# The low parts of 25 chunks of U made by a negated copy and an adding DMA instead of a subtraction on VectorE

## The chip, the cores and the metric

The kernel runs on one core of one Trainium2 chip. The metric is the time of one execution on the device, in microseconds, the median of three runs: 1719.38 us (1719.3 to 1720.42). Engines are named as in the profile: PE (matrix products), DVE (vector engine), ACT (activations, copies, and one DMA queue), POOL (GpSimd, and the DMA queue whose descriptors software writes), SP (a DMA queue).

## The reference

One decoder block on 512 tokens of width 1024, batch 1, in float32: a token mixer (a causal gated MLP, a sliding-window attention and two sigmoid gates, joined by an output projection) and then a retrieval layer over 16384 single-neuron experts. The change touches the retrieval layer alone:

```
q = (x @ w_pq) -> 8 heads of two halves; s1, s2 = halves . sub_keys      # (t, h, 128) each
v1, i1 = top_k(s1, 16); v2, i2 = top_k(s2, 16)
sc, ci = top_k(v1[..., :, None] + v2[..., None, :], 16)                  # 16 experts of each head
e = i1[ci // 16] * 128 + i2[ci % 16]
g = softmax(sc)
act = gelu(einsum(peer_u[e], x));  out = einsum(g * act, peer_v[e])
```

## The kernel before, in words

The first 459 us are the token mixer. Of the retrieval layer, 384 of the 512 tokens go a dense way: PE multiplies all 16384 rows of `peer_u` (128 chunks of 128 rows, called U here) with the tokens, Gelu is applied, and the result is multiplied with a dense matrix of weights that is zero except at each token's chosen experts; a second product with `peer_v` (V) gives the output. The last 128 tokens go by gathers of their own rows (`gather`, lines 662 to 691).

Every product in float32 precision is made of three products in a reduced format, with each operand split into a high part (the rounded value) and a low part (the rest): `mm3`, lines 59 to 65, issues hi·hi (L62), hi·h2Tlo (L63) and lo·h2Thi (L64) for each of eight slices of a chunk. PE works strictly in its order, so the third matmul of a chunk waits for the chunk's low part, and all behind it too.

The split of a chunk is `load_split2` (lines 445 to 459). SP loads `raw` (four buffers), ACT makes `hi` (three buffers) by a copy that rounds (L450), and the low part (three buffers) is a subtraction. POOL makes it while `last["pool"]` is set (L456), else DVE does (L458):

```
        if last.get("pool"):
            last["pool_lo"] = nc.gpsimd.tensor_sub(lo, raw, hi.bitcast(F32))
        else:
            last["dve"] = nc.vector.tensor_sub(lo, raw, hi.bitcast(F32))
```

`last["pool"]` is on from the query products to the end of the top-k; `end_topk` (line 818) clears it. The stage that follows, "the making of the dense weights", is `spread` (lines 607 to 658): for three tiles of 128 tokens and eight groups of 16 tokens in each, DVE builds four one-hot tensors of 128x2048 in 16 bit (`oh`, L631 to L635), PE multiplies them (32 short matmuls per group into `psg`, L643 and L644), ACT evicts the four results to `stg` (L645) and issues two DMAs that store them to DRAM (`Gd`, L656), and DVE keeps some of them in the resident tile `res` (L651, L653). Meanwhile 25 chunks of U, numbers 33 to 57, are computed as cover (`U_resident` and `U_chunk`, lines 693 to 717); the loop that pairs the two is at lines 858 to 867, five estimated microseconds of `spread` per chunk (`GPUMP`). `end_spread` (line 830) ends it, three more chunks of U follow, and then V.

The order in which each engine takes its instructions is not that of the code: a scheduler places them by its own estimates of when an operand is ready, and the order is fixed in the program. The gathers' first eight loads carry a note that puts them behind the last low part made on POOL (line 670, `behind(d, last["pool_lo"])`, which is an order on POOL's queue and no wait).

Of the kernel before, what the change touches and what calls it, by code (L numbers as in the profile page):

```python
# [8 lines left out]
F32 = mybir.dt.float32  # L9
# [4 lines left out]
AF = mybir.ActivationFunctionType  # L14
ALU = mybir.AluOpType
# [39 lines left out]
def block_kernel(ctx, tc, I, out):  # L55
    nc = tc.nc
# [52 lines left out]
    with ExitStack() as fr:  # L109
# [288 lines left out]
        for hh in range(2):  # L398
            for t in range(NT):
# [13 lines left out]
                for kh in range(2):  # L413
# [5 lines left out]
                    for k4 in range(4):  # L419
                        k = 4 * kh + k4  # L420
                        if k < NEV:
                            nc.scalar.activation(hf[:, k4, :], pt[:, k4 * P:(k4 + 1) * P], AF.Identity,
                                                 scale=G2c[:, k:k + 1], bias=B2c[:, k:k + 1])
# [11 lines left out]
    last = {}  # L435

    def behind(ins, other):

        tc.add_manual_dep(ins.ins, other.ins.name,
                          mybir.DependencyInfo(mybir.DependencyClass.NoSync, mybir.DependencyReason.DATA))  # L440
# [4 lines left out]
    def load_split2(src, nm, pool=None):  # L445
        raw = pw.tile([P, NK * P], F32, name=f"raw{nm}", tag="raw", bufs=4)
        last["dma"] = nc.sync.dma_start(raw, src)
        hi = (pool or pw).tile([P, NK * P], F32R, name=f"hi{nm}", tag="hi", bufs=1 if pool else 3)
        lo = (pool or pw).tile([P, NK * P], F32R, name=f"lo{nm}", tag="lo", bufs=1 if pool else 3)
        h = nc.scalar.activation(hi, raw, AF.Copy)  # L450
        if "expn" in last:
            last["expn"] -= 1
            if last["expn"] == 0:
                behind(last["exp"], h)
        if last.get("pool"):
            last["pool_lo"] = nc.gpsimd.tensor_sub(lo, raw, hi.bitcast(F32))  # L456
        else:
            last["dve"] = nc.vector.tensor_sub(lo, raw, hi.bitcast(F32))  # L458
        return Split(hi, lo)
# [56 lines left out]
    def query(h, half):  # L516
        nm = f"{h}_{half}"
        w = load_split2(I["w_pq"][2 * h + half], f"pq{nm}")
        ps = pu.tile([P, S], F32, name=f"psq{nm}", tag="mm", bufs=2)
        wv = Split(w.hi.rearrange("p (k c) -> p k c", k=NK), w.lo.rearrange("p (k c) -> p k c", k=NK))  # L520
        mm3(ps, [(wv[:, k, :], h2T[:, k, :]) for k in range(NK)])
        qt = tp.tile([P, S], F32, name=f"qt{nm}", tag="qt", bufs=2)
        nc.scalar.copy(qt, ps)
        return qt
# [168 lines left out]
    def U_resident(i):  # L693

        w = load_split2(I["uT"][i], f"U{i}")
        ps = pu.tile([P, SD], F32, name=f"psU{i}", tag="mm", bufs=2)
        wv = Split(w.hi.rearrange("p (k c) -> p k c", k=NK), w.lo.rearrange("p (k c) -> p k c", k=NK))
        last["U"] = mm3(ps, [(wv[:, k, :], h2T[:, k, 0:SD]) for k in range(NK)])
        slot, n = res["tile"][:, len(res["ids"]), :], res["spread"]
        if n < SD:  # L700
            nc.scalar.activation(slot[:, n:], ps[:, n:], AF.Gelu)
        if n:
            a = actp.tile([P, SD], F32, name=f"act{i}", tag="act", bufs=4)
            nc.scalar.activation(a[:, 0:n], ps[:, 0:n], AF.Gelu)
            nc.vector.tensor_mul(slot[:, 0:n], slot[:, 0:n], a[:, 0:n])
        res["ids"].append(i)

    def U_chunk(i, keep_act):
        w = load_split2(I["uT"][i], f"U{i}")
        ps = pu.tile([P, SD], F32, name=f"psU{i}", tag="mm", bufs=2)  # L710
        wv = Split(w.hi.rearrange("p (k c) -> p k c", k=NK), w.lo.rearrange("p (k c) -> p k c", k=NK))
        last["U"] = mm3(ps, [(wv[:, k, :], h2T[:, k, 0:SD]) for k in range(NK)])
        a = actp.tile([P, SD], F32, name=f"act{i}", tag="act", bufs=4)
        nc.scalar.activation(a, ps, AF.Gelu)
        if not keep_act:
            nc.scalar.dma_start(Ad[i], a)
        return a
# [100 lines left out]
    def end_topk():  # L818
        tk.close()
        last["pool"] = PLO > 1  # L820
        res["stack"] = ExitStack()
        rp = res["stack"].enter_context(tc.tile_pool(name="rp", bufs=1, side="right", reuse_waits="tile"))
        res["tile"] = rp.tile([P, NRES, SD], F32, name="res")
        res["ids"] = []
        res["first"] = cur[0] + 1
        res["spread"] = 0
        return
        yield

    def end_spread():  # L830
        done.append(1)
        last["pool"] = False
        return
        yield

    bg += [topk_last(), softmax(), end_topk(), spread(), end_spread()]
    gt = gather()
    n_g = 0
# [140 lines left out]
```

## Time and profile before

| what | us |
|---|---|
| median of three runs | 1719.38 |
| profiled execution, whole | 1727.59 |
| its span, first to last instruction | 1725.9 |
| PE busy in it | 1668.0 (97%) |
| DVE, ACT, POOL busy | 1353.8, 685.9, 481.5 |
| the stage of the change, from the last top-k to the first V chunk | about 720 to 886 |

The profiled execution is 8 us longer than the median of the runs; sums are made within it and their difference is carried to the median. A PE that is busy in the profile is not one at its peak, since matmuls overlap and their ends are modelled: how fast PE goes is read from the distance between the starts of its matmuls.

### The profile page before, as it was taken

To read this page: it belongs to the slowest core of one execution; us is meant where nothing else is said; L and a number is where in the kernel's file an instruction comes from. 1 tells how busy PE (TensorE), PEld (TensorE's weight loads), DVE (VectorE), ACT (ScalarE), POOL (GpSimd) and SP (SyncE) were. 2 spreads that over 40 slices of the span, in tenths; PEclk is the share of its full clock that TensorE was granted. 3 is DMA by queue.
4 is the path that set the end of the run, shared out by engine and by line. 5 is a ranking of instruction groups with operands and counts; after the bars stand their busy time and mean duration, and the time that the engine had idled before them with its cause. 6 is when DMAs were issued, how large, how long until landed. Compare 5 with 4: busy or idle time off the path is not lost.

```text
span 1725.9 us, 23559 instructions
## 1 busy us (share of the span) xinstructions
PE 1668.0 (97%) x8658; PEld 1442.8 (84%) x8658; DVE 1353.8 (78%) x2509; ACT 685.9 (40%) x1095; POOL 481.5 (28%) x334
## 2 busy tenths in 40 slices
PE   6999999999999999899999999999999999989997
PEld 3765777788788999899998789999999999978886
DVE  6467786454589999999978888778787888878787
ACT  3467632233343333355543233333333333333333
POOL 2000000000043455400014444444454545531202
PEclk9999999999999999999999999999999999999999
DMA  7602257642252355556699999999899999899982
GB/s 269 201 1 74 98 196 245 219 146 86 77 189 78 103 173 172 191 206 224 211 321 365 363 325 340 320 338 351 312 337 324 326 345 324 311 351 316 305 282 86
DMA packets 162071, 409.92 MB, mean 238 GB/s; under 512 B 22337, under 2 KB 69473, under 8 KB 161698
## 3 DMA queue, kind: packets, MB, share of 16 engines
q1 hardware_dynamic: 112178, 245.35, 42.3%
q0 software_dynamic: 36960, 134.50, 21.6%
q10 hardware_dynamic: 12816, 28.55, 4.3%
q8 instruction: 68, 1.11, 0.3%
q14 instruction: 49, 0.40, 0.1%
HBM read 377.07 MB, written 31.01 MB: 236 GB/s over the span
## 4 chain that ended last, share of the span: by engine, by line
PE 55%; DVE 18%; DMA 5%; issue 4%; POOL 2%; ACT 0%; SPq 0%; DVEq 0%; POOLq 0%; ACTq 0%
PE acc L801 8%; PE acc L800 8%; PE acc L797 8%; PE psU L64 7%; PE psU L62 6%; PE psU L63 6%; DMA wa<-in_w_ada_dram 2%; POOL ru L667 2%; DMA ru<-in_peer_u_dram,idx 1%; DMA rawV<-in_peer_v_dram 1%; PE pso L63 1%; PE pso L64 1%; PE psga L64 1%; PE psga L62 1%; PE pspa L64 1%
## 5 line engine op out<-in xcount | busy, mean ns | idle before, releaser
L64 PE MATMUL psU<-h2Thi,loU 128*128 128x384 f32 x1008 | 340.6, 338 | 5.4 <-DVE loU L458 5.3
L62 PE MATMUL psU<-h2Thi,hiU 128*128 128x384 f32 x1008 | 340.8, 338 | 0.0
L63 PE MATMUL psU<-h2Tlo,hiU 128*128 128x384 f32 x1008 | 339.3, 337 | 0.0
L797 PE MATMUL acc<-hiV,wh 128*128 128x512 f32 x768 | 300.1, 391 | 4.5 <-ACT wh L782 4.5
L800 PE MATMUL acc<-loV,wh 128*128 128x512 f32 x768 | 301.5, 393 | 1.5 <-DVE loV L458 1.5
L801 PE MATMUL acc<-hiV,wl 128*128 128x512 f32 x768 | 301.1, 392 | 0.3 <-DVE wl L783 0.3
L667 POOL DMA_INDIRECT ru<-in_peer_u_dram,idx x128 | 159.0, 1242 | 360.6 <-DVE ru L671 341.2
L680 POOL DMA_INDIRECT rv<-in_peer_v_dram,idx x128 | 176.4, 1378 | 247.9 <-DVE facc L686 226.6
L458 DVE TENSOR_TENSOR loV<-rawV,hiV 128x1024 fp32r<-128x1024 f32 x128 | 156.4, 1222 | 101.2 <-ACT hiV L450 100.9
L450 ACT ACTIVATE hiV<-rawV 128x1024 fp32r<-128x1024 f32 x128 | 135.1, 1055 | 224.2 <-PE psU L63 184.1
L450 ACT ACTIVATE hiU<-rawU 128x1024 fp32r<-128x1024 f32 x126 | 134.0, 1063 | 194.5 <-PE psU L63 105.5
L64 PEld LDWEIGHTS psU<-h2Thi,loU 128*128 128x128 f32 x1008 | 190.4, 189 | 7.7 <-DVE loU L458 7.6
L63 PEld LDWEIGHTS psU<-h2Tlo,hiU 128*128 128x128 f32 x1008 | 190.6, 189 | 2.6
L62 PEld LDWEIGHTS psU<-h2Thi,hiU 128*128 128x128 f32 x1008 | 190.4, 189 | 2.6
L797 PEld LDWEIGHTS acc<-hiV,wh 128*128 128x128 f32 x768 | 144.9, 189 | 33.7 <-ACT wh L782 5.1
L671 DVE SCALAR_TENSOR_TENSOR ru<-ru,h2n 128x1024 f32<-128x1024 f32 x128 | 154.4, 1221 | 22.0 <-DMA ru<-in_peer_u_dram,idx 21.8
L800 PEld LDWEIGHTS acc<-loV,wh 128*128 128x128 f32 x768 | 144.8, 189 | 32.0 <-DVE loV L458 3.1
L801 PEld LDWEIGHTS acc<-hiV,wl 128*128 128x128 f32 x768 | 144.8, 189 | 31.1 <-DVE wl L783 0.7
L686 DVE SCALAR_TENSOR_TENSOR facc<-rv,wg,facc 128x1024 f32<-128x1024 f32 x126 | 159.4, 1278 | 11.7 <-DMA rv<-in_peer_v_dram,idx 11.7
L456 POOL TENSOR_TENSOR lopq<-rawpq,hipq 128x1024 fp32r<-128x1024 f32 x16 | 40.7, 2544 | 325.1 <-ACT hipq L450 325.1
L782 ACT ACTIVATE wh<-wf 128x384 fp32r<-128x384 f32 x107 | 56.2, 526 | 183.4 <-DVE wf L778 100.5
L458 DVE TENSOR_TENSOR loU<-rawU,hiU 128x1024 fp32r<-128x1024 f32 x95 | 115.7, 1218 | 1.4 <-ACT hiU L450 1.4
(628 smaller groups left out, 2942.4 us busy)
## 6 DMA issues: line engine op xcount, KB each, us to landing
rawU<-in_uT_dram SPq DMA_DIRECT2D x128, 512.0 KB
rawV<-in_peer_v_dram SPq DMA_DIRECT2D x128, 512.0 KB
wa<-in_w_ada_dram SPq DMA_DIRECT2D x48, 512.0 KB
G<-Gd SPq DMA_DIRECT2D x11, 1536.0 KB
Gd<-stg ACTq DMA_DIRECT2D x24, 592.0 KB
rawpq<-in_w_pq_dram SPq DMA_DIRECT2D x16, 512.0 KB
Ad<-act ACTq DMA_DIRECT2D x38, 192.0 KB
ar<-Ad SPq DMA_DIRECT2D x9, 768.0 KB
```

What stands on the lines that cost most here:

```text
L62: nc.tensor.matmul(ps, l.hi, r.hi, start=(i == 0), stop=False)
L63: nc.tensor.matmul(ps, l.hi, r.lo, start=False, stop=False)
L64: last = nc.tensor.matmul(ps, l.lo, r.hi, start=False, stop=(i == n - 1))
L450: h = nc.scalar.activation(hi, raw, AF.Copy)
L458: last["dve"] = nc.vector.tensor_sub(lo, raw, hi.bitcast(F32))
L667: d = nc.gpsimd.indirect_dma_start(out=rows, out_offset=None, in_=I["peer_u"], in_offset=bass.IndirectOffsetOnAxis(ap=idx[:, s:s + 1], axi ...
L671: paced(nc.vector.scalar_tensor_tensor(rows, rows, 1.0, h2n, op0=ALU.mult, op1=ALU.mult, accum_out=wg[:, s:s + 1]))
L680: nc.gpsimd.indirect_dma_start(out=rows, out_offset=None, in_=I["peer_v"], in_offset=bass.IndirectOffsetOnAxis(ap=idx[:, s:s + 1], axis=0))
L686: paced(nc.vector.scalar_tensor_tensor(fa, rows, wg[:, s:s + 1], fa, op0=ALU.mult, op1=ALU.add))
L797: m = nc.tensor.matmul(acc, l.hi, r.hi, start=st, stop=False)
L800: nc.tensor.matmul(acc, l.hi, r.lo, start=False, stop=False)
L801: nc.tensor.matmul(acc, l.lo, r.hi, start=False, stop=sp_)
```

## The change

For chunks whose split is made between `end_topk` and `end_spread`, the low part is made in two steps: ACT writes the negated high part into `lo` (a copy with scale -1), and then POOL issues a DMA that adds `raw` to it, in SBUF, element by element.

```diff
-        if last.get("pool"):
+        if last.get("dma_lo"):
+            nc.scalar.activation(lo, hi.bitcast(F32), AF.Copy, scale=-1.0)
+            last["pool_lo"] = nc.gpsimd.dma_start(lo.bitcast(F32), raw, accum_op=ALU.add)
+        elif last.get("pool"):
             last["pool_lo"] = nc.gpsimd.tensor_sub(lo, raw, hi.bitcast(F32))
...
         res["ids"] = []
+        last["dma_lo"] = True
...
-        last["pool"] = False
+        last["pool"] = last["dma_lo"] = False
```

In the built program 25 subtractions leave DVE, 25 copies (L456 of the new code) join ACT and 25 DMAs (L457) join POOL. The scheduler also orders ACT, PE and DVE anew. In names, `hiU49` is the high part of chunk 49, `stg1_6` group 6 of the second tile of tokens, `psg1_6_3` its fourth product; the number at the end only tells buffers apart. The line numbers of the new code stand three higher from L456 on (an eviction is L648, a store L659, the short matmuls L646 and L647).

First place, ACT around groups 5 and 6 of the second tile. Before:

```order
L645 ACTIVATE stg1_5_7258<-psg1_5_3_7289 128x128x4
L656 DMA Gd_76<-stg1_5_7258 128x528
L656 DMA Gd_76<-stg1_5_7258 128x1184
L450 ACTIVATE hiU51_7582<-rawU51_7580 128x1024
L701 ACTIVATE res_6028<-psU48_7316 128x160
L704 ACTIVATE act48_7342<-psU48_7316 128x224
L645 ACTIVATE stg1_6_7345<-psg1_6_0_7346 128x128x4
L645 ACTIVATE stg1_6_7345<-psg1_6_1_7356 128x128x4
L645 ACTIVATE stg1_6_7345<-psg1_6_2_7366 128x128x4
L645 ACTIVATE stg1_6_7345<-psg1_6_3_7376 128x128x4
```

The same place on ACT after the change:

```order
L648 ACTIVATE stg1_5_7273<-psg1_5_3_7304 128x128x4
L450 ACTIVATE hiU49_7415<-rawU49_7413 128x1024
L659 DMA Gd_76<-stg1_5_7273 128x528
L659 DMA Gd_76<-stg1_5_7273 128x1184
L704 ACTIVATE res_6028<-psU48_7332 128x160
L707 ACTIVATE act48_7358<-psU48_7332 128x224
L648 ACTIVATE stg1_6_7361<-psg1_6_0_7362 128x128x4
L648 ACTIVATE stg1_6_7361<-psg1_6_1_7372 128x128x4
L648 ACTIVATE stg1_6_7361<-psg1_6_2_7382 128x128x4
L648 ACTIVATE stg1_6_7361<-psg1_6_3_7392 128x128x4
L456 ACTIVATE loU49_7416<-hiU49_7415 128x1024
```

Behind group 5 ACT made the high part of chunk 51 before and makes that of chunk 49 now, two chunks later in the sequence; the negated copy of chunk 49 stands behind the four evictions of group 6.

Second place, PE at chunk 49. Before, its 24 matmuls stand together behind group 6:

```order
L644 MATMUL psg1_6_3_7376<-oh2_1_6_7305,oh0_1_6_7303 128x128
L62 MATMUL psU49_7403<-h2Thi_2987,hiU49_7399 128x384
L63 MATMUL psU49_7403<-h2Tlo_2988,hiU49_7399 128x384
L64 MATMUL psU49_7403<-h2Thi_2987,loU49_7400 128x384
L62 MATMUL psU49_7403<-h2Thi_2987,hiU49_7399 128x384
```

Now PE takes two matmuls of the chunk, then the 32 of group 7, and then the other 22, the first of which reads the low part. The two ends of group 7:

```order
L647 MATMUL psg1_6_3_7392<-oh2_1_6_7320,oh0_1_6_7318 128x128
L62 MATMUL psU49_7420<-h2Thi_2987,hiU49_7415 128x384
L63 MATMUL psU49_7420<-h2Tlo_2988,hiU49_7415 128x384
L646 LDWEIGHTS oh0_1_7_7406
L646 MATMUL psg1_7_0_7450<-oh1_1_7_7407,oh0_1_7_7406 128x128
```

```order
L647 LDWEIGHTS oh0_1_7_7406
L647 MATMUL psg1_7_3_7480<-oh2_1_7_7408,oh0_1_7_7406 128x128
L64 MATMUL psU49_7420<-h2Thi_2987,loU49_7416 128x384
L62 MATMUL psU49_7420<-h2Thi_2987,hiU49_7415 128x384
L63 MATMUL psU49_7420<-h2Tlo_2988,hiU49_7415 128x384
```

So between group 6, which ACT must evict ahead of the negated copy, and the first use of the low part, PE has two long and 32 short matmuls to do.

Third place, the end of the stage on POOL. Before, the first gathers (`ru`) follow the low part of chunk 32; now they follow the 25 adding DMAs:

```order
L457 DMA loU55_7950<-rawU55_7947 128x1024
L457 DMA loU56_8036<-rawU56_8033 128x1024
L457 DMA loU57_8122<-rawU57_8119 128x1024
L670 DMA ru0_8344<-in_peer_u_dram,idx_8342 128x1024
L670 DMA ru1_8375<-in_peer_u_dram,idx_8342 128x1024
```

The gathers moved from the start of the stage to its end.

## Rows read from the trace of the kernel before

**Rows 1.** The page's part 4, shares of the chain that ended last, by engine.

```profile
PE 55%; DVE 18%; DMA 5%; issue 4%; POOL 2%; ACT 0%; SPq 0%; DVEq 0%; POOLq 0%; ACTq 0%
```

**Rows 2.** Windows: us, busy time per engine (instructions), PE clock, DMA share, GB/s.

```profile
700.00:720.00 20.00, 18.98 (x111) 18.63 (x109) 19.52 (x49) 9.33 (x12) 6.39 (x3) 1.00 0.37 127
720.00:886.00 166.00, 159.47 (x1397) 153.24 (x1398) 158.39 (x193) 88.63 (x174) 5.87 (x4) 0.98 0.64 229
885.00:910.00 25.00, 25.00 (x125) 22.31 (x124) 18.49 (x28) 10.40 (x16) 9.09 (x8) 1.00 1.06 363
910.00:1000.00 90.00, 85.39 (x375) 70.61 (x374) 75.18 (x114) 29.06 (x38) 45.22 (x37) 0.98 0.98 364
```

**Rows 3.** Waits of PE from 690 to 900: us, times, longest.

```profile
PE psg L643 <- DVE oh L635: 2.6, 3, 1.4
PE psU L64 <- DVE loU L458: 2.5, 2, 2.1
PE ptg L615 <- DVE gs L595: 2.3, 1, 2.3
```

**Rows 4.** Instructions by line from 720 to 886: busy us, mean ns, idle before.

```profile
L645 ACT ACTIVATE stg<-psg 128x512 f32<-128x512 f32 x96 | 49.8, 608 | 13.2 <-PE psg L644 13.2
L458 DVE TENSOR_TENSOR loU<-rawU,hiU 128x1024 fp32r<-128x1024 f32 x28 | 34.0, 1217 | 1.2 <-ACT hiU L450 1.2
L450 ACT ACTIVATE hiU<-rawU 128x1024 fp32r<-128x1024 f32 x25 | 26.7, 1068 | 30.7 <-PE psU L63 26.1 <-DVE oh L634 4.6
L701 ACT ACTIVATE res<-psU 128x240 f32<-128x240 f32 (+19 forms) x21 | 7.4, 354 | 12.4 <-PE psU L64 12.4
```

**Rows 5.** Timeline of PE: start, us, line; two long, two short matmuls.

```profile
760.39 0.33 PE L64 MATMUL psU<-h2Thi,loU 128*128 128x384 f32 x1
760.56 0.33 PE L62 MATMUL psU<-h2Thi,hiU 128*128 128x384 f32 x1
...
763.03 0.22 PE L643 MATMUL psg<-oh,oh 128*128 128x128 f16 x1
763.09 0.22 PE L644 MATMUL psg<-oh,oh 128*128 128x128 f16 x1
```

**Rows 6.** Timeline of ACT, a group's two stores issued.

```profile
845.70 0.81 ACTq L656 DMA_DIRECT2D Gd<-stg  x2
```

**Rows 7.** DMA of the stage, 720 to 886: packets and bytes.

```profile
DMA packets 11966, 37.98 MB, mean 229 GB/s; under 512 B 1321, under 2 KB 1956, under 8 KB 11951
```

**Rows 8.** Chain in order of time: start, us; DMA pieces, issue to use.

```profile
282.28 4.25 DMA wa<-in_w_ada_dram
...
977.79 9.72 DMA ru<-in_peer_u_dram,idx
```

**Rows 9.** Timeline of POOL, the two copies inside SBUF.

```profile
58.94 0.76 POOL L206 DMA_DIRECT2D kd<-kd  x1 [24.52 <-ACT kd L204]
59.69 0.57 POOL L207 DMA_DIRECT2D kd<-kd  x1
```

**Rows 10.** DMA from 57 to 62: share in 40 slices; queue: packets, MB, share.

```profile
DMA  8610000000000000000000000098951049898000
...
q0 software_dynamic: 96, 0.26, 23.9%
```

**Rows 11.** Timeline of POOL, first and last of four gathers issued beside DVE's work.

```profile
720.12 1.76 POOL L667 DMA_INDIRECT ru<-in_peer_u_dram,idx  x1 [10.23 <-DVE idx L664]
...
724.94 1.97 POOL L667 DMA_INDIRECT ru<-in_peer_u_dram,idx  x1 [0.30 <-issue]
```

**Rows 12.** Line L667 in the whole span: ns least, median, most.

```profile
L667 POOL DMA_INDIRECT ru<-in_peer_u_dram,idx x128: 933/1012/1967, 720.1 to 1228.5; - x128
```

**Rows 13.** Timeline of PE about 988: a wait, and matmuls behind it.

```profile
986.88 0.34 PE L63 MATMUL psU<-h2Tlo,hiU 128*128 128x384 f32 x1
990.04 0.44 PE L64 MATMUL psU<-h2Thi,loU 128*128 128x384 f32 x1 [2.82 <-DVE loU L458]
...
991.38 0.50 PE L62 MATMUL psU<-h2Thi,hiU 128*128 128x384 f32 x1
```

## Prediction

> **What bounds the kernel now.** I read first the shares of the chain that ended last [rows 1]: PE has 55%, DVE 18%, DMA 5%. Then the windows about the stage that the change touches [rows 2]. From 720 to 886 PE is busy 159.47 of 166.00 us and DVE 158.39, so both look full. Which of them is late is told by the waits of PE [rows 3]: in all it waited 7.4 us for DVE (2.6 for one-hots, 2.5 for low parts, 2.3 for the softmax), which agrees with the idle time of the windows, 6.5 us in 720 to 886 and 1.0 in 700 to 720. The granted clock of the stage is 0.98, a further 0.02 x 166 = 3.3 us. So the most that a faster DVE can give is 7.5 + 3.3 = 10.9 us, although the change takes three times that off DVE. The reader is to see here that a busy share of 95% on DVE is no measure of what its relief is worth: PE is nearly full beside it.
>
> How fast PE goes is read from starts [rows 5]: a long matmul every 0.17 us, a short one every 0.057. A chunk of U is 24 long ones, 4.15 us; a group of the dense weights is 32 short ones, 1.82 us.
>
> **The change part by part.** Removed: 25 subtractions of 1.217 us [rows 4] on DVE, 30.4 us. At most the 10.9 us above come of it. I take 6: the waits for one-hots and low parts go (5.1), and some of the wait for the softmax, which stood behind two subtractions; the clock's 3.3 us I leave, since new waits of PE would lower it too.
>
> Added on ACT: 25 negated copies. The trace has none; the nearest row is the copy of the same tile that makes the high part, 1.07 us [rows 4], so 26.7 us more on an engine that is busy 88.6 of 166 [rows 2]; with stores issued at 0.81 us for two [rows 6], 24 times, that is 88.6 + 26.7 + 19.4 = 135. ACT as a whole is not the bound.
>
> Added on POOL: 25 DMAs. An issue is bounded by 0.57 [rows 9] and 1.97 us [rows 11]; I take the median of the gathers, 1.0 [rows 12]. Nothing but gathers is queued behind them.
>
> Added on the DMA engines: 25 x 0.524 MB = 13.1 MB to the 37.98 MB of the stage [rows 7], at a share that is 0.64 now [rows 2]. An adding DMA is not in the trace, so I bound its landing. A plain load of 0.524 MB took 4.25 us from issue to use [rows 8]; 0.524 MB at the 364 GB/s of a full ring [rows 2] is 1.44 of it, so 2.8 us are fixed. The only copies inside SBUF, issued by POOL, kept their queue at 23.9% of 16 engines for 5 us with 0.26 MB [rows 9, 10]: 19.1 engine-us, or 2.4 us for 0.524 MB. Low end 2.8 (the transfer itself hidden), high end the 9.7 us of a gather of that size in a full ring [rows 8]. I take 2.8 + 2.4 = 5.2, by the copy that is nearest in kind. At that price 25 of them fill 60 us, a share of 0.36, and the ring would stand at 1.00.
>
> What is late next: the low part itself. Before, it came 1.2 us after the high part, and ACT made the high part up to three chunks ahead. Now the order on PE has to cover the copy, the issue and the landing. In the new order I counted, for each of the 25 chunks, what PE has to do between the last of its groups that ACT must see ahead of the negated copy and the first matmul that reads the low part. That cover is 2 long and 32 short matmuls for chunk 49, the place shown, 2.2 us. It is 4.3 for chunks 39 and 50 (4 long, 64 short); 5.3 for 41; 6.3 for 40 and 48; 6.7 to 7.1 for 38, 42 and 47; 5.9 for 57; 7.3 to 8.6 for 51 to 56; 8.0 to 16 for the other nine.
>
> The chain to be covered has three forms, with 0.61 for the last eviction, 1.07 for a copy [rows 4], 0.81 for two issues [rows 6]:
> - eviction, negated copy, issue, landing: 0.61 + 1.07 + 1.0 + 5.2 = 7.9. Short by 0.8 at 38, 1.1 at 47, 0.5 at 48 (47's wait counts for it), 5.7 at 49.
> - eviction, high part, two issues, negated copy, issue, landing: 9.8. Short by 5.5 at 39 (40 lies within that wait), and by 1.2 to 2.5 at each of 51 to 56, 10.2 in all; since each of these chains begins ahead of the wait before it, a wait serves two of them, 5.1. The same at 57: 3.9, half of it 2.0.
> - after a chunk's result: two activations of 0.35 [rows 4] and then the copy, 8.0 at chunk 50, short by 3.7; at 41 also an eviction, two issues and two high parts, 11.5, short by 6.2 (42 lies within).
>
> Sum 30.6 us. It moves by 9.5 us for each us of landing: six chunks in full, seven by half.
>
> A wait of PE is followed by a slower PE: after 2.82 us for a low part the next matmuls took 0.50 us instead of 0.33, and the clock of that stretch is 0.98 of 90 us, 1.8 us lost [rows 2, 13]. Four new waits are longer than that; I take 4 us (0 to 7).
>
> Moved: the first four gathers go on POOL's queue behind the 25 DMAs, from a stage with a share of 0.64 to the end of it. DVE reads them after the stage, so their latency is hidden, but 2.1 MB fall near the stretch from 885 to 1000, where the ring is full and PE lost 4.6 of 90 us [rows 2]: 2.1 MB at 364 GB/s are 5.8 us of the ring. I take 2. The loads of U on SP wait for a buffer that an adding DMA frees instead of DVE; four buffers at six us a chunk hide that at a landing of 5.2, and no longer at 9.7.
>
> Sum: 30.6 + 4 + 2 - 6 = 30.6 us. The profiled execution would go from 1727.6 to 1758; the runs lie 8 us below it, so the median goes from 1719.4 to 1750.
>
> The Trainium skill, Collectives: The Full Stack, section on the speed of ReduceScatter, says that an add in a DMA costs a second read of the source side, and that this and not the adder halves its rate. No row here shows an adding DMA. By it the 2.4 us of transfer become 4.8, the landing 7.6, and the time 1750 + 2.4 x 9.5 = 1773; this is the second case below. The Trainium skill, DMA: Bandwidth & Descriptors, section Anatomy of one DMA, gives for a DMA of POOL's queue 2.0 us and its bytes over 436 GB/s, an estimate of 3.2 us here. By that the waits sum to about 15 and the time is 1731, the third case.
>
> **Rivals.**
> 1. The ring is the bound. An add reads two operands and a copy one; twice the 60 us of transfers gives 106 + 120 of the stage's 166 us; then landings go toward 9.7 and the loads of U and the stores, on which the evictions wait, come late too. For it: 0.64 is the share before anything is added. Against: a ring at 1.06 still moved 363 GB/s. Landings of 7.6 to 9.7 add 23 to 43 us: 1773 to 1793.
> 2. The landing is nearer the low end, about 3.1: the copies of rows 9 and 10 were over within 3 us of the first issue, though of 0.13 MB each. The chains are 5.8, 7.7, 5.9 and 9.4 long, and 39, 41, 49, 50 and 57 are short by 3.4, 4.1, 3.6, 1.6 and 0.9; with 1 for the clock and 2 for the gathers, less 6: 1730.
> 3. Not slower: the landing hides almost whole. Decisive is a landing of 2.2 us with all of the 10.9 us won: the waits are then 2.5, 3.2, 2.7 and 0.7, some 9, the gathers 2, and it is a draw at 1719. Below 2.2 it is faster, down to 1711. For it: PE's cover is 8 us or more at half of the chunks. Against: the 4.25 us of a plain load.
> 4. The change frees DVE and nothing waits for the new path: 1709. This is the end of case 3, and I give it no share of its own.
>
> **How the numbers follow.** Chances: forecast (landing 4 to 6.5, 1738 to 1764) 0.38; ring 0.24; short landing 0.19; not slower 0.19, of which faster by over 0.2% is 0.11 and within 0.2% is 0.08. 0.2% (3.4 us) is about what a measurement of this kernel can tell from no change. Slower: 0.81. The range is from 1713, which leaves out the lower part of case 3, to 1792, which leaves out the worst of case 1; my own case alone is 1738 to 1764.
>
> **What would show it.** Right: PE waits for `loU` at the L64 of chunks 39, 41, 49 and 50 with 3 to 7 us each, DVE's busy time falls by 30 us, and most of DVE's idle time follows from PE's delay; the stage from 720 grows by 25 to 30 us, and what follows V's start keeps its length. The size is wrong if the waits are there and the landing differs: 9.5 us for each. The mechanism is wrong if PE's waits for `loU` sum to under 10 us, or if PE waits instead for evictions behind stores (the ring) or for one-hots (DVE still late).

## The result and the profile after

The change is slower. The median of four runs is 1763.6 us (1760.56 to 1768.68) against 1719.9 us (1719.3 to 1723.05) for the kernel before; the ratio is 1.0253, with a 95% interval from 1.0222 to 1.0284. The forecast was 1750, its range 1713 to 1792. The profiled execution took 1766.13 us with a span of 1764.4, which is 38.5 more than the span before.

The chain that ended last, by engine, in the page of the changed kernel, answers to [rows 1]:

```profile
PE 61%; DVE 16%; issue 11%; DMA 7%; POOL 3%; ACT 1%; SPq 0%; DVEq 0%; POOLq 0%; ACTq 0%
```

DVE's share fell from 18 to 16 and DMA's rose from 5 to 7, with 11% of "issue", time in which the chain's engine waits for nothing that the profile shows; from 815 to 860, in the chain in order of time, that stands between POOL's issues of adding DMAs. Where the time is lost, the windows tell. Columns as in [rows 2]:

```profile
700.00:720.00 20.00, 18.46 (x108) 18.09 (x106) 19.45 (x46) 11.34 (x14) 7.32 (x5) 1.00 0.58 173
720.00:930.00 210.00, 180.37 (x1462) 170.11 (x1463) 144.15 (x182) 116.88 (x207) 28.48 (x31) 0.96 0.88 257
930.00:960.00 30.00, 25.07 (x101) 19.90 (x100) 18.42 (x29) 8.76 (x12) 11.05 (x9) 0.89 0.96 337
960.00:1045.00 85.00, 81.73 (x368) 69.09 (x367) 70.49 (x104) 27.34 (x36) 42.55 (x34) 0.98 0.96 358
```

Up to 720 PE had lost nothing: it had begun 3301 matmuls by then before, and 3303 now. From there PE is idle for 30 us of 210, where it was idle for 6.5 of 166. DVE, nearly full before, is busy for 144 of the 210: it has been relieved, and no other engine gained by it. The stage ends with the first product of V, in the timelines of PE of before and of after:

```profile
894.43 0.39 PE L797 MATMUL acc<-hiV,wh 128*128 128x512 f32 x1
```

```profile
925.82 0.39 PE L800 MATMUL acc<-hiV,wh 128*128 128x512 f32 x1
```

That is 31.4 of the 38.5 us. What PE waits for from 690 to 940 (us in total, times, longest), the answer to [rows 3]:

```profile
PE psU L64 <- DMA loU<-rawU: 20.8, 12, 5.0
PE psg L646 <- DVE oh L638: 5.7, 4, 3.0
PE ptg L618 <- DVE gs L598: 2.3, 1, 2.3
PE psU L62 <- ACT hiU L450: 1.6, 5, 0.4
PE psg L646 <- ACT stg L648: 0.6, 3, 0.2
```

In sum 31.0 us instead of 7.4. The granted clock is 0.96 over 210 us, 8.4 us lost, instead of 3.3. Both together are 28.7 of the 31.4. Windows cut at the first product of V close the account: from 720 PE is busy for 167.9 us and idle for 6.5 before, busy for 176.2 and idle for 29.6 now. That is 23.1 us more of idle time and 8.3 more for the same matmuls, of which the clock's mean explains 5.1; the rest was not traced further. Single waits in PE's timeline, with the idle time and its releaser in brackets:

```profile
755.33 0.44 PE L64 MATMUL psU<-h2Thi,loU 128*128 128x384 f32 x1 [0.72 <-DMA loU<-rawU]
...
766.09 0.23 PE L646 MATMUL psg<-oh,oh 128*128 128x128 f16 x1 [2.96 <-DVE oh L638]
769.19 0.45 PE L64 MATMUL psU<-h2Thi,loU 128*128 128x384 f32 x1 [0.70 <-DMA loU<-rawU]
776.19 0.44 PE L64 MATMUL psU<-h2Thi,loU 128*128 128x384 f32 x1 [2.89 <-DMA loU<-rawU]
783.37 0.22 PE L646 MATMUL psg<-oh,oh 128*128 128x128 f16 x1 [1.81 <-DVE oh L638]
820.56 0.44 PE L64 MATMUL psU<-h2Thi,loU 128*128 128x384 f32 x1 [2.43 <-DMA loU<-rawU]
...
840.69 0.69 PE L64 MATMUL psU<-h2Thi,loU 128*128 128x384 f32 x1 [5.00 <-DMA loU<-rawU]
...
909.39 0.44 PE L64 MATMUL psU<-h2Thi,loU 128*128 128x384 f32 x1 [2.21 <-DMA loU<-rawU]
```

Counted along PE's order, the low parts waited for in these rows are those of chunks 38, 39, 40, 47, 49 and 57. How the longest comes about is seen in ACT's timeline ahead of it, and in POOL's:

```profile
827.11 1.08 ACT L450 ACTIVATE hiU<-rawU 128x1024 fp32r<-128x1024 f32 x1
...
831.62 0.30 ACT L704 ACTIVATE res<-psU 128x160 f32<-128x160 f32 x1 [3.43 <-PE psU L64]
831.82 0.35 ACT L707 ACTIVATE act<-psU 128x224 f32<-128x224 f32 x1
832.10 2.06 ACT L648 ACTIVATE stg<-psg 128x512 f32<-128x512 f32 x4
834.03 1.08 ACT L456 ACTIVATE loU<-hiU 128x1024 fp32r<-128x1024 f32 x1
```

```profile
835.40 0.87 POOL L457 DMA_DIRECT2D loU<-rawU  x1 [14.86 <-PE psg L647]
```

The high part of chunk 49 is ready at 828.2. Its negated copy stands in ACT's order behind two activations and four evictions that wait for PE itself, and starts at 834.03; POOL issues at 835.40, and the sum lands so that PE goes on at 840.69, 5.3 us after the issue began. (The row names PE as what ended POOL's wait; ACT's copy, which the DMA must follow, ended at 835.11.) Over all 25, the view of line L457 gives the time from the start of the issue, which it includes, to the landing (least, median, most):

```profile
DMA to landing us min/median/max: 4.5/6.7/9.2
```

The three costs by line from 720 to 930 (columns as in [rows 4]):

```profile
L456 ACT ACTIVATE loU<-hiU 128x1024 fp32r<-128x1024 f32 x23 | 24.5, 1066 | 3.1 <-ACT hiU L450 2.7
L457 POOL DMA_DIRECT2D loU<-rawU x23 | 20.0, 868 | 163.9 <-ACT loU L456 114.4 <-PE psg L647 27.9 <-DMA Gd<-stg 20.2
...
L654 DVE TENSOR_TENSOR res<-res,stg 128x336 f32<-128x336 f32 (+19 forms) x24 | 8.8, 367 | 34.9 <-ACT stg L648 18.5 <-ACT res L704 16.4
```

DVE is idle for 34.9 us ahead of one kind of small product, which waits for ACT; the one-hots behind it in DVE's order come late with it, as at 773.8, where DVE had waited 7.2 us before it could start on one-hots that PE then waits for at 783. ACT in turn had waited for PE's products (52.4 us ahead of its own `res` in this stretch). So the relieved DVE still makes PE wait, 5.7 us where it was 2.6.

After the stage, another 5.5 us are lost where V starts: from its first product to its 22nd chunk the trace has 106.7 us, and that of before 101.2. The longest wait of PE there, in its timeline, and the wait of ACT behind it, summed from 925 to 1045:

```profile
950.89 0.79 PE L800 MATMUL acc<-hiV,wh 128*128 128x512 f32 x1 [4.46 <-ACT hiV L450]
```

```profile
ACT hiV L450 <- DMA rawV<-in_peer_v_dram: 22.1, 4, 11.2
```

In the kernel before, that wait of ACT sums to 8.1 us from 894 to 1014. The loads of V come late in a ring at 0.96 that now also carries the moved gathers; that the gathers are the cause is not shown (see run 4). The remaining 1.6 us of the 38.5 are spread over what follows.

### The profile page after: what moved, and what is told of

The parts are those of the page before. It is cut to its first block, busy times and chain, and to the rows that moved or that the text cites. A ratio compares the mean times of both kernels' runs of the same rounds, so it can differ in the third digit from the quotient of the medians.

```text
span 1764.4 us, 23642 instructions
## 1 busy us (share of the span) xinstructions
PE 1676.4 (95%) x8658; PEld 1448.7 (82%) x8658; DVE 1330.3 (75%) x2484; ACT 709.8 (40%) x1120; POOL 502.9 (29%) x359
## 4 chain that ended last, share of the span: by engine, by line
PE 61%; DVE 16%; issue 11%; DMA 7%; POOL 3%; ACT 1%; SPq 0%; DVEq 0%; POOLq 0%; ACTq 0%
PE acc L804 8%; PE acc L803 8%; PE acc L800 8%; PE psU L64 6%; PE psU L62 6%; PE psU L63 6%; DMA wa<-in_w_ada_dram 3%; POOL ru L670 2%; PE pss L246 1%; DMA rawV<-in_peer_v_dram 1%; PE psgv L62 1%; PE psgv L64 1%; PE psgv L63 1%; DVE wa L147 1%; PE pso L64 1%
## 5 line engine op out<-in xcount | busy, mean ns | idle before, releaser
L64 PE MATMUL psU<-h2Thi,loU 128*128 128x384 f32 x1008 | 343.4, 341 | 23.5 <-DMA loU<-rawU 20.8
L800 PEld LDWEIGHTS acc<-hiV,wh 128*128 128x128 f32 x768 | 145.5, 189 | 38.5 <-ACT hiV L450 4.9
L147 DVE SCALAR_TENSOR_TENSOR wa<-wa,cs 128x1024 f32<-128x1024 f32 x48 | 62.7, 1309 | 42.3 <-DMA wa<-in_w_ada_dram 35.1
```

Source lines behind the costliest of these rows:

```text
L64: last = nc.tensor.matmul(ps, l.lo, r.hi, start=False, stop=(i == n - 1))
L800: m = nc.tensor.matmul(acc, l.hi, r.hi, start=st, stop=False)
```

## The experiments

The kernel before took 1719.9 to 1723.2 us (medians) in the comparisons. "V starts" is the first product of V in PE's timeline, in the profiled execution: 894.4 before, 925.8 after.

| run | median us | ratio to before, 95% | V starts |
|---|---|---|---|
| changed kernel | 1763.6 | 1.0253 [1.0222, 1.0284] | 925.8 |
| 1 whole path beside DVE | 1764.8 | 1.0241 [1.0224, 1.0258] | 926.5 |
| 2 ACT's copies, DVE waits | 1745.2 | 1.0123 [1.0106, 1.0140] | 910.9 |
| 3 negated copy first | 1752.3 | 1.0161 [1.0133, 1.0189] | 917.9 |
| 4 gathers early | 1767.8 | 1.0268 [1.0244, 1.0292] | 936.2 |
| 5 DMAs beside, one scratch | 1762.2 | 1.0225 [1.0191, 1.0259] | 927.5 |
| 6 ACT's copies beside | 1740.5 | 1.0103 [1.0065, 1.0141] | 911.8 |
| 7 thin DMAs | 1742.0 | 1.0110 [1.0078, 1.0141] | 902.5 |
| 8 plain copies | 1751.0 | 1.0167 [1.0138, 1.0197] | 914.2 |
| 9 new PE order alone | 1745.7 | 1.0141 [1.0124, 1.0158] | 915.4 |
| 10 ACT's copies, old PE order | 1736.5 | 1.0083 [1.0066, 1.0099] | 904.2 |
| 11 DMAs beside, two scratches | 1730.8 | 1.0057 [1.0038, 1.0077] | 892.9 |
| 12 POOL subtracts | 1758.0 | 1.0214 [1.0194, 1.0233] | 926.3 |

One execution of run 6 took 9436 us, unlike every other, and is left out. Only some runs keep an order: PE's is that of the changed kernel in runs 4, 8 and 9, and that of the kernel before in runs 5, 10 and 11; in runs 1, 2, 3, 6, 7 and 12 the scheduler made PE a new one. ACT's and DVE's orders agree too in runs 4 and 8 (with the changed kernel) and in run 5 (with the kernel before), ACT's alone in run 11. Each diff is against the changed kernel, but that of run 12, which is against the kernel before; "..." marks what is left out. "Theory" at first was the prediction's: the low part's chain of copy, issue and landing is longer than PE's order covers. The rivals were the traffic, ACT's time and the new order. Line numbers move with each edit; the names of the operands tell the place.

**Run 1, the whole path, nobody waiting for it.**

```diff
             nc.scalar.activation(lo, hi.bitcast(F32), AF.Copy, scale=-1.0)
-            last["pool_lo"] = nc.gpsimd.dma_start(lo.bitcast(F32), raw, accum_op=ALU.add)
+            nc.gpsimd.dma_start(last["scr"], raw, accum_op=ALU.add)
+            last["dve"] = nc.vector.tensor_sub(lo, raw, hi.bitcast(F32))
...
```

> The whole added path runs, but nothing of PE waits for it: ACT makes the 25 negated copies into the low tiles, POOL issues the 25 adding DMAs into a scratch tile that nobody reads, and VectorE then overwrites the low tiles by its subtraction, as before. Theory (PE waits for a late landing): the time falls back to that of before plus what the moved gathers and the fuller ring cost at V's start, about 6 us: 1722 to 1730, and PE's waits for loU sum to under 8 us. Rival (the 13.1 MB more in the ring, or ACT's 26.6 us more, slow the stage by themselves): 1740 or more, with no loU wait that names a DMA.

1764.8: as slow as the change, with no wait of PE on a DMA. This looked like the rival, but POOL's waits show another cause, of the experiment's own making:

```profile
POOL scr L457 <- DMA scr<-rawU: 140.4, 21, 9.8
```

All 25 DMAs add into one tile, so each waits for the one before, and the raw tiles are held. The run decides nothing about the ring; run 11 mends it.

**Run 2, ACT's copies alone.**

```diff
             nc.scalar.activation(lo, hi.bitcast(F32), AF.Copy, scale=-1.0)
-            last["pool_lo"] = nc.gpsimd.dma_start(lo.bitcast(F32), raw, accum_op=ALU.add)
+            last["dve"] = nc.vector.tensor_sub(lo, raw, hi.bitcast(F32))
```

> Only the 25 negated copies on ACT are added to the kernel before; the low parts still come from VectorE, which overwrites them, and there is no DMA. Theory: ACT has room, 1718 to 1724. Rival (ACT is the bound of the stage): a good part of its 26.6 us shows, 1735 or more. The difference of this run and the one with the DMAs beside it is the price of the traffic alone: 6 by the theory, 20 or more if the ring is the bound.

1745.2, the rival's number, although ACT is busy for only 115 of the 191 us from 720 on. PE's waits:

```profile
PE psU L64 <- DVE loU L457: 10.7, 8, 2.8
```

DVE here has to wait for ACT's copy before it overwrites it, which burdens a full DVE; run 6 takes that away.

**Run 3, the chain made shorter.**

```diff
+        if last.get("dma_lo"):
+            nc.scalar.activation(lo, raw, AF.Copy, scale=-1.0)
+            last["pool_lo"] = nc.gpsimd.dma_start(lo.bitcast(F32), raw, accum_op=ALU.add)
         h = nc.scalar.activation(hi, raw, AF.Copy)
...
```

> The changed kernel with ACT's two copies of a chunk exchanged: the negated copy comes first, straight from the raw tile, so the adding DMA starts 1.07 us earlier and the high part is made 1.07 us later. Theory (landing not covered by PE's order, 12 waits of PE for loU with 20.8 us): each of the 12 waits shrinks by up to 1.07 us, 8 to 12 us in all, if waits for hiU grow by less than 4: 1752 to 1760. Rival (order of the groups or the ring, not the length of this chain): 1762 to 1767.

1752.3, as the theory had it: 11.3 less than the change by the medians, 16 by the ratios to the kernel before, and V starts 7.9 us earlier. Waits of PE from 690 to 940:

```profile
PE psU L64 <- DMA loU<-rawU: 14.3, 7, 3.3
PE psU L62 <- ACT hiU L453: 3.2, 3, 1.9
PE psg L648 <- DVE oh L640: 2.4, 2, 2.2
```

The low parts' waits fall by 6.5, the high parts' grow by 1.6, the one-hots' fall by 3.3. The prediction's slope was 9.5 us for each us of the chain; 1.07 us gave 8 in the stage of the trace and 11 or more in the runs. PE's order is a new one here, so how much of it the shorter chain gave was not separated.

**Run 4, gathers ahead of the adding DMAs.**

```diff
-            last["pool_lo"] = nc.gpsimd.dma_start(lo.bitcast(F32), raw, accum_op=ALU.add)
+            nc.gpsimd.dma_start(lo.bitcast(F32), raw, accum_op=ALU.add)
```

> The changed kernel, but the first eight gathers keep their place behind the last subtraction of POOL and so go out ahead of the 25 adding DMAs, as before; nothing else moves on PE or ACT. Theory: the 6 us that V's start has lost come at least in part from these 2.1 MB, 1758 to 1762, and the time from the stage's start to its end stays. Rival (V's start is late because its weights and dense values are loaded into a ring that the last adding DMAs still fill): 1763 to 1766.

1767.8, no gain, and above both expected ranges. POOL's timeline, and PE's longest wait:

```profile
721.27 0.94 POOL L670 DMA_INDIRECT ru<-in_peer_u_dram,idx  x1 [0.30 <-issue]
722.21 1.06 POOL L457 DMA_DIRECT2D loU<-rawU  x1
```

```profile
730.57 0.69 PE L64 MATMUL psU<-h2Thi,loU 128*128 128x384 f32 x1 [13.02 <-DMA loU<-rawU]
```

The first low part now stands behind gathers on POOL's queue, and they behind DVE's indices; PE waits 13.0 us for it. V starts 10 us later. But from there to V's 22nd chunk the trace has 98.7 us, less than either kernel: the loss at V's start is gone. That fits a price of the moved gathers, but does not show it, since V starts later here and its loads have more time. Run 3 has the gathers at the end too, and takes 101.9 us there; run 2 has them early and takes 104.8. So what the 5.5 us are is open; the old place of the gathers, ahead of the adding DMAs, costs more.

**Run 5, the DMAs alone, in the old order of PE, ACT and DVE.**

```diff
-            nc.scalar.activation(lo, hi.bitcast(F32), AF.Copy, scale=-1.0)
-            last["pool_lo"] = nc.gpsimd.dma_start(lo.bitcast(F32), raw, accum_op=ALU.add)
+            last["dve"] = nc.vector.tensor_sub(lo, raw, hi.bitcast(F32))
+            nc.gpsimd.dma_start(last["scr"], raw, accum_op=ALU.add)
...
```

> The kernel before, with only the 25 adding DMAs put beside it: they add the raw tiles into a scratch tile that nobody reads, ACT makes no negated copy, the low parts come from VectorE, and PE, ACT and VectorE have word for word the order of the kernel before. So it prices the traffic and POOL's issues alone. The run with the whole path beside VectorE's subtractions took 1764.8 and that with ACT's copies alone 1745.2, both about before plus 42 and 22. Theory (the fuller ring slows loads, and stores on which evictions wait): 1737 to 1747. Rival (traffic is harmless, and the order and the waits cost the time): 1722 to 1730.

1762.2, more than either expected. ACT's waits from 720 to 910:

```profile
ACT hiU L450 <- DMA rawU<-in_uT_dram: 58.8, 13, 6.7
```

This is run 1's flaw: one scratch tile, DMAs in single file (POOL waits 137.7 us for them, in 20 waits), raw tiles held for as long. It shows only that raw tiles held longer starve ACT.

**Run 6, ACT's copies into a scratch tile.**

```diff
-            nc.scalar.activation(lo, hi.bitcast(F32), AF.Copy, scale=-1.0)
-            last["pool_lo"] = nc.gpsimd.dma_start(lo.bitcast(F32), raw, accum_op=ALU.add)
+            last["dve"] = nc.vector.tensor_sub(lo, raw, hi.bitcast(F32))
+            nc.scalar.activation(last["scr"].bitcast(F32R), hi.bitcast(F32), AF.Copy, scale=-1.0)
...
```

> The kernel before, with only the 25 negated copies of ACT, into a scratch tile that nobody reads, and no DMA. In the earlier run of this kind VectorE's subtraction overwrote ACT's copy and so had to wait for it; here it does not. Theory (ACT's 26.6 us and the order that the scheduler makes of them cost time by themselves, in late evictions and high parts): 1738 to 1747 as there. Rival (there it was only VectorE's added wait, with VectorE nearly full): 1722 to 1729.

1740.5 (three runs of 1738.7 to 1741.3). ACT's copies, with the new order of PE that came with them, cost 18 us here with no DMA and no wait on them. PE waits for what ACT and, behind it, DVE now make later:

```profile
PE psU L64 <- DVE loU L456: 8.1, 9, 2.0
PE psU L62 <- ACT hiU L450: 4.5, 5, 2.5
```

**Run 7, the path without its bytes.**

```diff
-            last["pool_lo"] = nc.gpsimd.dma_start(lo.bitcast(F32), raw, accum_op=ALU.add)
+            last["pool_lo"] = nc.gpsimd.dma_start(lo[:, 0:8].bitcast(F32), raw[:, 0:8], accum_op=ALU.add)
```

This kernel leaves nearly all of the addition out.

> The changed kernel with adding DMAs of 8 columns out of 1024 (32 bytes a partition), so that nearly all of the addition is left out: copies, issues and PE's waits for the DMA stay, the 13.1 MB go. Theory (bytes in a full ring make landings long and the loads and stores late): the landing falls from 6.7 to under 4 us, PE's waits for loU from 20.8 to under 10, 1735 to 1747. Rival (the fixed part of a DMA behind the copy is the cost): landing 5 or more, waits 15 or more, 1752 to 1764.

1742.0, as the theory had it; PE's waits for the low part:

```profile
PE psU L64 <- DMA loU<-rawU: 7.5, 6, 2.5
```

The stage is only 8.0 us longer than before, not 31.4. But PE's order is not the changed kernel's, so the 23.4 us between them are the price of the bytes and of the order together; run 8 has the order fixed. From V's first product to its 22nd chunk it takes 106.4 us, as in the change.

**Run 8, a copy in place of the add.**

```diff
-            last["pool_lo"] = nc.gpsimd.dma_start(lo.bitcast(F32), raw, accum_op=ALU.add)
+            last["pool_lo"] = nc.gpsimd.dma_start(lo.bitcast(F32), raw)
```

This kernel leaves the addition out.

> The changed kernel with the DMAs as plain copies of the raw tile into the low tile, so the addition is left out, in the same order on every engine and with the same waits. It prices the second read. Rival taken from the documents (an add reads its source side twice): landing 1.5 to 2.4 us shorter than 6.7, time down by 10 or more, 1740 to 1754. Theory (the fixed part and the share of the ring set the landing, not the adder): landing within 0.7 us of 6.7, 1756 to 1766.

1751.0, with 8.0 us of waits for low parts instead of 20.8, in the same order of every engine: the theory of this run fell, and adding itself costs some 13 us (V starts 11.6 us earlier without it). The view has no landings for this run, but the place at chunk 49 shows the shorter one:

```profile
833.56 0.54 POOL L457 DMA_DIRECT2D loU<-rawU  x1 [12.60 <-PE psg L647]
```

```profile
837.33 0.44 PE L64 MATMUL psU<-h2Thi,loU 128*128 128x384 f32 x1 [3.48 <-DMA loU<-rawU]
```

PE goes on 3.8 us after the issue began, where it was 5.3 with the add. Queue 0 from 740 to 860, when no gather is on it (packets, MB, share of 16 engines), of the change and of this run:

```profile
q0 software_dynamic: 1988, 7.28, 32.6%
```

```profile
q0 software_dynamic: 2160, 7.87, 16.4%
```

That is 0.326 x 120 x 16 / 7.28 = 86 engine-us per MB with the add and 40 without, 2.15 times as much; a low part of 0.524 MB keeps 16 engines for 2.8 us instead of 1.3. The Trainium skill, Collectives: The Full Stack, section on the speed of ReduceScatter, says that the add needs two reads on the source side, and that this halves its rate; these rows agree, with 2.15.

**Run 9, PE's new order alone.** A table of the runs of matmuls, read from the changed kernel's order, ties each run's first matmul behind the last of the one ahead. What the engines have to do is otherwise that of the kernel before, but for clearing a scratch tile that nobody reads; ACT's and DVE's work was placed anew beside this order.

```diff
+    for run in ORDER:
...
+            behind(seq[k][a], prev)
```

> The kernel before with nothing added on ACT, POOL or the DMA engines, and VectorE's subtractions as they were, but with PE held, matmul for matmul, to the order that the changed kernel has in the stage. It prices that order by itself. Theory (the order is no cost of its own, since it only follows from the later low parts): 1719 to 1726. Rival (groups of the dense weights back to back ask VectorE for one-hots faster than it makes them, and the looser order makes PE wait): 1732 or more, with waits for one-hots of 10 us or more.

1745.7, the rival's case. This order costs 24 us when DVE still has the subtractions; PE's waits:

```profile
PE psg L660 <- DVE oh L652: 20.4, 10, 5.5
PE ptg L632 <- DVE gs L612: 2.3, 1, 2.3
PE psU L78 <- DVE loU L471: 2.1, 1, 2.1
```

Groups that stand back to back ask for one-hots faster than DVE makes them, 4.9 us a group. In the change DVE has 30 us less to do, so this price is not a part of its 31.4 as it stands; what part of it is left there was not measured.

**Run 10, ACT's copies in PE's old order.**

```diff
-            nc.scalar.activation(lo, hi.bitcast(F32), AF.Copy, scale=-1.0)
-            last["pool_lo"] = nc.gpsimd.dma_start(lo.bitcast(F32), raw, accum_op=ALU.add)
+            last["dve"] = nc.vector.tensor_sub(lo, raw, hi.bitcast(F32))
+            nc.scalar.activation(last["scr"].bitcast(F32R), hi.bitcast(F32), AF.Copy, scale=-1.0)
...
```

PE is held to the order of the kernel before by a table as in run 9.

> The kernel before with the 25 negated copies of ACT into a scratch tile, as in the run that took 1740.9, but with PE held to the order of the kernel before; no DMA. Theory (1.07 us more in ACT's line ahead of the next high part or eviction makes those late at many places, whatever PE's order): 1732 to 1742. Rival (the 19 us of that run came from PE's new order): 1720 to 1727.

1736.5, the theory's case: 26.6 us more of ACT's time in its line cost 14.5 us with PE in its old order (what else ACT and DVE do was placed anew).

```profile
PE psU L76 <- ACT hiU L465: 8.7, 4, 2.7
PE psU L78 <- DVE loU L471: 5.0, 3, 2.6
```

**Run 11, the DMAs alone, with two scratch tiles.**

```diff
-            nc.scalar.activation(lo, hi.bitcast(F32), AF.Copy, scale=-1.0)
-            last["pool_lo"] = nc.gpsimd.dma_start(lo.bitcast(F32), raw, accum_op=ALU.add)
+            last["dve"] = nc.vector.tensor_sub(lo, raw, hi.bitcast(F32))
+            last["two"].reverse()
+            nc.gpsimd.dma_start(last["two"][0], raw, accum_op=ALU.add)
...
```

> As the run with the 25 adding DMAs alone beside VectorE's subtractions (1762.2), with PE and ACT in the order of the kernel before, but with two scratch tiles in turn. In the former run each DMA waited for the landing of the one before, since both wrote the same tile, and ACT waited 58.8 us for raw tiles that these DMAs held. Theory (that queue of DMAs was the cost there; the bytes alone cost the stage little): 1722 to 1734, ACT's waits for raw loads under 15 us. Rival (13.1 MB of adding traffic slow the ring so that loads and stores come late in any case): 1745 or more.

1730.8, the theory's case. V even starts 1.5 us earlier than before in the profiled executions, though the ring is full (share 1.00):

```profile
720.00:930.00 210.00, 199.79 (x1593) 186.84 (x1592) 194.44 (x244) 106.05 (x199) 41.71 (x40) 1.00 1.00 315
```

The view of its DMAs' line has landings of 5.3, 9.3 and 10.5 us (least, median, most), longer than the change's. The early start is not a gain of the ring: the granted clock of this stretch is 1.00, worth some 3 us against 0.98, and PE's waits from 720 to V's first product sum to 8.3 us instead of 7.4. So a full ring costs this stage little as long as nobody waits for its landings; the whole run is 8.8 us longer at the median.

**Run 12, the same relief of DVE without ACT and DMA:** POOL subtracts.

```diff
-            last["pool_lo"] = nc.gpsimd.tensor_sub(lo, raw, hi.bitcast(F32))
+            d = nc.gpsimd.tensor_sub(lo, raw, hi.bitcast(F32))
+            if not last.get("stage"):
+                last["pool_lo"] = d
...
-        last["pool"] = PLO > 1
+        last["stage"] = True
```

> The kernel before with the 25 subtractions of the stage on POOL (2.4 us each in the trace) and not on VectorE; no copies on ACT and no DMAs, and the gathers keep their place. VectorE is relieved of the same 30 us. Theory (the relief is worth at most 10.9 us, and POOL is 1.2 us later with a low part): 1712 to 1722. Rival (POOL's later low parts make PE wait as the DMAs did, 25 times up to 1.2 us): 1725 to 1740.

1758.0, worse than the rival, and mostly by another way. PE waits once for a low part of POOL, and otherwise for DVE, whose own instructions are longer:

```profile
PE psg L645 <- DVE oh L637: 26.8, 15, 4.4
PE psU L64 <- POOL loU L456: 7.1, 1, 7.1
```

```profile
L637 DVE TENSOR_TENSOR oh<-oh,gT 128x2048 f16<-128x2048 f16 x24 | 41.9, 1744 | 0.4
```

```profile
L456 POOL TENSOR_TENSOR loU<-rawU,hiU 128x1024 fp32r<-128x1024 f32 x25 | 77.1, 3092 | 96.6 <-ACT hiU L450 91.2 <-DMA Gd<-stg 5.4
```

The same one-hot product took 1.217 us before, and a subtraction on POOL 2.46 in the stage ahead of this one. In this run's timelines the 30 one-hot products that meet no subtraction of POOL take 1.21 to 1.23 us, and the 66 that overlap one 1.83 in the mean. PE's order is a new one here too, so the 36 us are not the price of this alone. No version tried beats the kernel before.

## Why the prediction was right, and where not

It forecast slower by waits for late low parts. The trace shows these waits; run 8, with every order as in the change, takes away 12.8 us of them and 12.6 of the time; run 11 shows that the same traffic without such waits costs the stage little. Runs 3 and 7 point the same way, with PE's order changed. The rest of the loss is less well known. By the prediction's own terms, within the profiled executions:

| term | forecast | measured |
|---|---|---|
| PE's waits for low parts | 30.6 | 20.8 |
| what DVE's relief gives | -6 | +0.6 |
| waits for high parts and evictions | 0 | 2.2 |
| clock in the stage | 4 | 5.1 |
| moved gathers, V's start | 2 | 5.5 |
| rest of the stage, and what follows V's start | 0 | 4.3 |
| sum | 30.6 | 38.5 |

The sum is nearer than its terms: the waits for low parts came out 9.8 us under the forecast, and the other terms 17.7 over it. That part is luck. Of the signs that were set, the waits sum to over 10 us as asked, but of the four chunks named only 49 waited 3 us or more, and what follows V's start grew by 7.1 us where it was to keep its length.

- **The chain and its sites.** Forecast at chunk 38 0.8, at 39 and 40 5.5, 41 6.2, 47 1.1, 48 0.5, 49 5.7, 50 3.7, 51 to 56 5.1, 57 2.0. Measured 0.72, 3.59, none, 2.43, 0.55, 5.00, 1.35, 4.94 and 2.21, which is the 20.8. Counting cover along PE's order gave nearly every place. The sizes at 39 and 41 failed because PE was late there already: the waits of 2.96 and 1.81 us for one-hots, at 766 and 783, stand in the cover of these two and gave their low parts the time. The landings of 39, 41, 49 and 50 were also among the shorter ones (4.5 to 5.3 us from the start of the issue, by POOL's issues and PE's order), under the 6.2 forecast.
- **The landing.** "I take 2.8 + 2.4 = 5.2" behind an issue of 1.0, 6.2 in all; the median from the start of the issue to the landing is 6.7, with 0.87 of issue in it. The transfer was near by two errors, which is luck: a copy takes 1.3 us of 16 engines, not 2.4, and the add doubles it to 2.8. By the rule of the Trainium skill's Collectives: The Full Stack I had priced 4.8, since the copy that it doubles was too dear. The Trainium skill, DMA: Bandwidth & Descriptors, section Anatomy of one DMA, led to an estimate of 3.2 us; the shortest landing of the change, 4.5 with its issue, is 3.6 behind it, in a ring at 0.88.
- **The step that failed: "the waits for one-hots and low parts go (5.1)".** Of the 6 us that I credited to DVE, the old low-part waits of 2.5 went, and the one-hots' waits rose by 3.1. Nothing of the 10.9 that were the upper bound came: DVE stood behind ACT for 34.9 us, and PE's new order puts groups back to back, which run 9 shows to be dear in one-hots with DVE full. How much each of the two did here was not separated.
- **"ACT as a whole is not the bound"** is true of its busy time (117 of 210) and still wrong as a price of nothing: run 10 lost 14.5 us to the copies in the old order with DVE full. In the change little of this shows as waits for high parts (1.6); how much is in the negated copies' late places, as at chunk 49, was not separated. For that the changed kernel with PE held to the old order would be needed, which wasn't run.
- **Ring as the bound (0.24).** The add does keep the DMA engines twice as long, as this rival had it, but the ring stood at 0.88, and run 11 had it full with the stage no longer. By that run the bytes cost through the landings that PE waits for: the add's share of them is 11.6 us of the stage, by run 8, and nearly all of the bytes some 23, by run 7, whose order of PE differs.
- **The median.** I carried over the 8 us by which the profiled execution of before lies above its median. The one of after lies 2.5 above; the difference is 5.7 of the 13.6 us by which 1750 missed, and 7.9 come from the sum.

## What to carry to other kernels

Work moved off a busy engine is worth only the waits that this engine causes, and the new path is to be priced by its whole chain against the cover that the consumer's order gives, site by site; that found most of the places here, though not the sizes. A copy on an engine with room to spare is not free when it stands in that engine's line ahead of results that others wait for. To price traffic alone, give it destinations that do not make its transfers wait for each other; two of these runs (1 and 5) measured that instead. To price one part of a change, hold every engine's order, or say that it moved.

## What the hardware showed unexpectedly

An adding DMA inside SBUF kept the DMA engines 2.15 times as long per byte as a plain copy, and its issue took POOL 0.87 us where the copy's took 0.54. With POOL subtracting beside it, DVE's 16-bit products of 128x2048 took 1.56 to 1.74 us (means by line) instead of 1.22, and POOL's subtraction 3.09 instead of 2.46; products that met no subtraction kept their 1.22. A DMA ring at a share of 1.00 and 315 GB/s did not lengthen the stage in the profiled execution of run 11, at a granted clock of 1.00 where it was 0.98 before.
